# A 2048 x 2048 x 2048 matrix product with layer norm: the order of the first loads and products

## The chip, the cores and the metric

The kernel runs on one core of one Trainium2 chip. The metric is the device time of one execution in microseconds. A core has several engines, each with its own instruction queue: TensorE (PE in the profile; its weight loads are shown apart as PEld) does the matrix products, VectorE (DVE) and ScalarE (ACT) work elementwise, GpSimd (POOL) and SyncE (SP) here mostly issue transfers. An engine works through its queue in order and waits on semaphores that other engines or transfers raise. Transfers (DMA) are issued from a queue and then run beside the engines.

## The reference

```python
x = np.matmul(a, b)                       # a, b: 2048 x 2048, float32
mean = np.mean(x, axis=-1, keepdims=True)
var = np.var(x, axis=-1, keepdims=True)
normalized = (x - mean) / np.sqrt(var + eps)
return (gamma * normalized + beta).astype(np.float32)
```

The product has 16 x 16 x 4 = 1024 steps of 128 rows of A, 128 of K and 512 columns of B, each one TensorE instruction (called a product below). The inputs arrive as float32 and are multiplied as float16 with float32 sums.

## The kernel before

A is cut into 16 row tiles of 128 rows, B into 16 k tiles of 128 rows and 4 column blocks of 512 columns. Four k tiles make a chunk (KC = 4). Three things have to happen before a product can run: B's piece is loaded into a staging buffer (pool `stg`, 6 buffers of 1024 columns, or two halves of 512) and cast to float16 by VectorE; the row tile of A is loaded and cast likewise; and A is turned, since TensorE wants it with K on the partitions. In the first stage `turn` (L238) does that with TensorE: four transposes for each row tile and chunk into a PSUM bank, then one ScalarE copy back to SBUF. Products accumulate in PSUM, which has 8 banks; one bank holds one sum of 128 x 512 (`acc`), the result of one turn, or the target `warm` of the zero products. A bank goes to its next user when the engine that reads it is done.

All order is written out by hand (`manual_schedule`): each engine's queue is the order of the Python calls.

The first R = 5 row tiles (0 to 4) are worked together while B arrives, so that a piece of B serves five products. Their row pairs are [0, 1], [2, 3] and [4] (`pairs`, L208). The stages are:

- Opening (L269 to L286): block 0, k tiles 0 to 3, for the five rows, in the order in which the first pieces land: A row tile 0, B k tile 0, A row tiles 1 to 4, B k tiles 1, 2, 3 (`arrivals`, L163). `filler(n)` (L234) issues n products of zeros into the bank `warm`. After the stage the sums are put aside to SBUF by ScalarE (`put_aside`), which frees the banks.
- Blocks 1 and 2, k tiles 0 to 3 (L289 to L296), put aside likewise.
- Block 3, called MAIN, over all 16 k tiles (L299 to L315). Beside it the rows' next chunks are turned (`spots`, and the `turn` at L310). In its last chunk the rows finish one by one; `evacuate` (L90) copies the sum to SBUF on ScalarE and takes its statistics on VectorE, and `bring` (L250) issues the load and the cast of the next pieces of B (k tiles 4 to 15 of blocks 0, 1 and 2, 18 pieces in all).
- The rest of blocks 0, 1 and 2 (L318 to L328, L411 to L415): k tiles 4 to 15, added to what was put aside by VectorE (`add_rest`, L263).
- Row tiles 5 to 15 one after the other (L416 to L432), with all of B in SBUF; their A tiles are loaded with a cast from GpSimd's queue and turned by a transposing DMA from SP's queue. The normalisation of finished rows runs on VectorE from a backlog beside the products. After the last row only its own normalisation is left (`finish_row`).

The loads of the first stage are all issued on SP in the order of L216 to L230: the arrivals, blocks 1 and 2 of chunk 0, row pair 0 of chunk 1, and then, for each chunk c, the two pieces of block 3 (`load_b2`, two k tiles each, 512 KB) with the row pairs of chunk c + 1 between them (`load_pair`, 512 KB, or 256 KB for the single row tile 4). A load waits until its staging buffer has been cast, so both the issues on SP and the casts on VectorE follow this order.

Of the kernel before, what the change touches and what calls it, by code (L numbers as in the profile page):

```python
# [16 lines left out]
def kernel(  # L17
# [15 lines left out]
    n_kt = K // P  # L33
# [3 lines left out]
    KC = 4  # L37
    KW = KC * P
    n_kc = n_kt // KC
    R = 5  # L40
    ASIDE, MAIN = (0, 1, 2), 3
# [31 lines left out]
    def bank(name):  # L73
        return psum.tile([P, NB], FP32, tag="ps", name=name)
# [4 lines left out]
    def at(i):  # L79
        return pair[i // 2][:, i % 2]  # L80

    def mm(i, q, kt, first, last):
        if (i, q) not in acc:
            acc[i, q] = bank(f"acc{i}_{q}")
        nc.tensor.matmul(  # L85
            acc[i, q], at(i)[:, kt, :], b16[:, kt, ds(q * NB, NB)],
            start=first, stop=last,
        )

    def evacuate(i, q):  # L90
        if xs[i] is None:
            xs[i] = xpool.tile([P, N], FP32, tag="x", name=f"x{i}")
            bnst[i] = stat.tile([P, n_nb, 6], FP32, tag="bnst", name=f"bnst{i}")
        qs = ds(q * NB, NB)
        nc.scalar.copy(xs[i][:, qs], acc[i, q])  # L95
        nc.vector.bn_stats(bnst[i][:, q, :], xs[i][:, qs])  # L96
# [85 lines left out]
    def load_a1(i, c):  # L182
        st = half_stage()
        nc.sync.dma_start(st, a[ts(i, P), ts(c, KW)])  # L184
        a16_room(i, c)
        nc.vector.tensor_copy(a16_of[i, c], st)  # L186

    def load_a2(i, c):
        st = stg.tile([P, 2, NB], FP32, tag="st", name=f"sta{i}_{c}")
        nc.sync.dma_start(  # L190
            st, a[ds(i * P, 2 * P), ts(c, KW)].rearrange("(t p) k -> p t k", p=P))
        for m in (0, 1):
            a16_room(i + m, c)
        nc.vector.tensor_copy(held["a"][:, ds(i % KC, 2), :], st)  # L194
# [6 lines left out]
    def load_b2(k, q):  # L201
        st = stg.tile([P, 2, NB], FP32, tag="st", name=f"stb{q}_{k}")
        nc.sync.dma_start(
            st, b[ds(k * P, 2 * P), ds(q * NB, NB)].rearrange("(t p) n -> p t n", p=P))
        nc.vector.tensor_copy(b16[:, k:k + 2, ds(q * NB, NB)], st)  # L205
        return st

    pairs = [list(range(i, min(i + 2, R))) for i in range(0, R, 2)]  # L208

    def load_pair(j, c):  # L210
        if len(pairs[j]) == 2:
            load_a2(pairs[j][0], c)
        else:
            load_a1(pairs[j][0], c)
# [7 lines left out]
    for c in range(n_kc):  # L222
        load_b2(c * KC, MAIN)
        if c + 1 < n_kc:
            if c > 0:
                load_pair(0, c + 1)
            load_pair(1, c + 1)
        load_b2(c * KC + 2, MAIN)
        if c + 1 < n_kc:
            load_pair(2, c + 1)  # L230

    warm = bank("warm")

    def filler(n, to=None):  # L234
        for _ in range(n):
            nc.tensor.matmul(warm if to is None else to, zeros[:, 0:P], zeros, start=True, stop=True)  # L236

    def turn(rows, c):  # L238
        n = len(rows)
        t_ps = psum.tile([P, n, KC, P], FP16, tag="ps", name=f"tps{rows[0]}_{c}")  # L240
        for m, i in enumerate(rows):
            for j in range(KC):
                nc.tensor.transpose(t_ps[:, m, j, :], a16_of[i, c][:, ts(j, P)], ident)  # L243
        i0 = rows[0]
        nc.scalar.copy(  # L245
            pair[i0 // 2][:, ds(i0 % 2, n), ds(c * KC, KC), :], t_ps)
# [3 lines left out]
    def bring(n):  # L250
        for _ in range(n):
            k, q = later.pop(0)
            st = load_b2(k, q)
            if not later:
                nc.gpsimd.tensor_copy(gate, st[:, 0, 0:1])

    def put_aside(p, q):
        if xs[p] is None:
            xs[p] = xpool.tile([P, N], FP32, tag="x", name=f"x{p}")
            bnst[p] = stat.tile([P, n_nb, 6], FP32, tag="bnst", name=f"bnst{p}")  # L260
        nc.scalar.copy(xs[p][:, ds(q * NB, NB)], acc.pop((p, q)))  # L261
# [10 lines left out]
    mm(0, 0, 0, True, False)  # L272
    filler(1)
    turn([1], 0)
    filler(1)
    for i in range(2, R):
        filler(1)
        turn([i], 0)
        mm(i - 1, 0, 0, True, False)
    mm(R - 1, 0, 0, True, False)  # L280
    for kt in range(1, KC):
        filler(2 if kt == 1 else 0)
        for p in range(R):
            mm(p, 0, kt, False, kt == KC - 1)
            if kt == KC - 1:
                put_aside(p, 0)  # L286
# [12 lines left out]
    spots = {(0, 4): 0, (1, 1): 1, (1, 4): 2}  # L299
    for h in (0, 1):  # L300
        for p in range(R):
            for kt in (2 * h, 2 * h + 1):
                mm(p, MAIN, kt, kt == 0, False)
            if (h, p) in spots:
                turn(pairs[spots[h, p]], 1)
    for kt in range(KC, n_kt - KC):
        for p in range(R):
            mm(p, MAIN, kt, False, False)
        if kt % KC > 0:
            turn(pairs[kt % KC - 1], kt // KC + 1)  # L310
    for p, n in enumerate((0, 1, 0, 1, 1)):
        for kt in range(n_kt - KC, n_kt):
            mm(p, MAIN, kt, False, kt == n_kt - 1)
        bring(n)
        evacuate(p, MAIN)  # L315
# [152 lines left out]
```

## Time and profile before

| | us |
|---|---|
| median of 3 runs (lowest, highest) | 246.81 (246.68, 247.35) |
| profiled execution: its own time | 246.63 |
| profiled execution: span from first to last instruction | 244.6 |
| TensorE products, busy | 223.5 of 236.8 |
| VectorE busy | 175.2 |
| ScalarE busy | 52.6 |
| zero products (L236), 27: 19 in the opening, 8 behind the last row | 9.0 |
| transposes on TensorE (L243), 80 | 6.8 |
| casts of B in pieces of 1024 columns (L205), 30 of them, mean of one | 0.687 |

The page of a profile gives the span in parts: the busy time of each engine, the load of the DMA engines over time, the chain of work that ended last (followed back from the last instruction, at each step to what released it), and groups of instructions by line with what ended the idle time before them. The trace can also be asked for an engine's instructions in order of time (the timeline: start, duration, engine, line, operation, what it writes and reads, how many; in brackets the idle time before and what ended it), for all waits of one engine, and for the busy time of each engine in a stretch. Matmuls are pipelined: a product's bar is 0.38 us long, though one starts every 0.216 us.

Over the first 45 us the DMA engines move some 385 to 400 GB/s without a pause. The granted clock of TensorE is 1.00 in every stretch from 5.1 us on that was asked for.

### The profile page before, as it was taken

How to read it: one execution, taken by the hardware profiler on the slowest of the kernel's cores; microseconds unless marked ns; L12 is line 12 of the kernel's file. 1: busy time of each engine (PE TensorE's matmuls, PEld its weight loads, DVE VectorE, ACT ScalarE, POOL GpSimd, SP SyncE). 2: the span in 40 equal slices, each digit the busy share in tenths (PEclk: the TensorE clock that was granted, in tenths of full speed). 3: DMA queues.
4: the chain of work that ended last, by engine and by line, in shares of the span. 5: the costliest groups of instructions: out<-in, count | busy, mean ns of one | idle time of the engine just before them, and what ended most of it. 6: DMA issues, size and time to landing. Idle time of an engine off the chain costs nothing.

```text
span 244.6 us, 2975 instructions
## 1 busy us (share of the span) xinstructions
PE 236.8 (97%) x1137; PEld 108.0 (44%) x1137; DVE 175.2 (72%) x310; ACT 52.6 (21%) x96; POOL 7.2 (3%) x17
## 2 busy tenths in 40 slices
PE   7899999999999999999999999999999999999982
PEld 2344555444444444444444444444444444444430
DVE  1554554949997679999999995937557391947873
ACT  2457446400000011112111211112111211112100
POOL 0000000000300100000000000000000000000000
PEclk9999999999999999999999999999999999999996
DMA  4999999999999999899979897683907144120405
GB/s 125 398 386 385 388 387 385 316 357 375 331 271 179 158 131 201 196 316 205 263 189 283 147 298 222 149 200 71 256 4 190 68 123 137 74 97 0 175 1 172
DMA packets 41190, 52.64 MB, mean 215 GB/s; under 512 B 24404, under 2 KB 24404, under 8 KB 40920
## 3 DMA queue, kind: packets, MB, share of 16 engines
q1 hardware_dynamic: 39592, 46.68, 60.5%
q0 software_dynamic: 1584, 5.77, 15.4%
q8 instruction: 9, 0.15, 0.2%
q14 instruction: 5, 0.04, 0.0%
HBM read 35.67 MB, written 16.78 MB: 214 GB/s over the span
## 4 chain that ended last, share of the span: by engine, by line
PE 94%; DMA 2%; DVE 1%; ACT 0%; SPq 0%; issue 0%
PE acc L85 90%; DMA st<-in_a_dram 2%; PE tps L243 2%; PE w L380 1%; PE warm L236 1%; DVE x L390 0%; DVE bnst L364 0%; DVE x L367 0%; ACT at L245 0%; DVE a16s L186 0%; SPq L198 0%; PE nm_ps L375 0%; SPq L184 0%; DVE mv L102 0%; ACT lead L376 0%
## 5 line engine op out<-in xcount | busy, mean ns | idle before, releaser
L85 PE MATMUL acc<-b,at 128*128 128x512 f16 x1024 | 223.5, 379 | 0.7 <-DVE b L199 0.4
L85 PEld LDWEIGHTS <-at 128*128 128x128 f16 x1024 | 99.7, 98 | 119.7 <-ACT at L245 2.1
L96 DVE BATCH_NORM_STATS2 bnst<-x 128x6 f32<-128x512 f32 x48 | 33.0, 690 | 34.1 <-ACT x L95 33.9
L95 ACT COPY x<-acc 128x512 f32<-128x512 f32 x48 | 28.1, 586 | 107.8 <-PE acc L85 107.8
L117 DVE SCALAR_TENSOR_TENSOR x<-x,rstd,beta_b 128x512 f32<-128x512 f32 x61 | 43.1, 748 | 0.5
L111 DVE SCALAR_TENSOR_TENSOR x<-x,mv,gamma_b 128x512 f32<-128x512 f32 x60 | 42.1, 743 | 0.0
L205 DVE CAST b<-stb 128x1024 f16<-128x1024 f32 x30 | 20.4, 687 | 13.0 <-DMA stb<-in_b_dram 12.9
L106 ACT ACTIVATE sq<-ve 128x1 f32<-128x1 f32 x16 | 3.2, 203 | 55.5 <-DVE ve L104 55.5
L245 ACT COPY at<-tps 128x512 f16<-128x512 f16 (+1 forms) x14 | 10.8, 768 | 14.1 <-PE tps L243 14.0
L265 DVE TENSOR_TENSOR x<-acc,x 128x512 f32<-128x512 f32 x15 | 10.3, 686 | 3.0 <-PE acc L85 2.7
L266 DVE BATCH_NORM_STATS2 bnst<-x 128x6 f32<-128x512 f32 x15 | 10.4, 694 | 0.5
L236 PE MATMUL warm<-zeros 128*128 128x512 f16 x27 | 9.0, 463 | 1.2 <-DVE zeros L152 1.2
L340 POOL DMA_DIRECT2D a<-in_a_dram x11 | 6.4, 587 | 91.6 <-DMA at<-a 91.3
L261 ACT COPY x<-acc 128x512 f32<-128x512 f32 x15 | 7.6, 606 | 6.0 <-PE acc L85 6.0
L243 PEld LDWEIGHTS <-a16s 128*128 128x128 f16 x80 | 5.4, 98 | 4.7 <-DVE a16s L186 2.4
L243 PE MATMUL tps<-ident,a16s 128*128 128x128 f16 x80 | 6.8, 219 | 0.4 <-DVE a16s L186 0.3
L194 DVE CAST a16s<-sta 128x1024 f16<-128x1024 f32 x6 | 4.2, 694 | 4.0 <-DMA sta<-in_a_dram 4.0
L186 DVE CAST a16s<-st 128x512 f16<-128x512 f32 x8 | 3.4, 427 | 5.0 <-DMA st<-in_a_dram 4.8
L236 PEld LDWEIGHTS <-zeros 128*128 128x128 f16 x27 | 2.9, 113 | 4.6 <-issue 2.2
L102 DVE BATCH_NORM_AGGREGATE mv<-bnst 128x2 f32<-128x24 f32 x16 | 4.2, 264 | 0.5
L199 DVE CAST b<-st 128x512 f16<-128x512 f32 x4 | 1.7, 427 | 1.8 <-DMA st<-in_b_dram 1.8
L104 DVE TENSOR_TENSOR ve<-mv,eps_t 128x1 f32<-128x1 f32 x16 | 2.6, 160 | 0.5
(26 smaller groups left out, 16.9 us busy)
## 6 DMA issues: line engine op xcount, KB each, us to landing
stb<-in_b_dram SPq DMA_DIRECT2D x30, 512.0 KB, 6.5
out_dram<-x SPq DMA_DIRECT2D x30, 512.0 KB, 3.1
a<-in_a_dram POOLq DMA_DIRECT2D x11, 512.0 KB, 6.9
sta<-in_a_dram SPq DMA_DIRECT2D x6, 512.0 KB, 6.6
st<-in_a_dram SPq DMA_DIRECT2D x8, 256.0 KB, 6.3
st<-in_b_dram SPq DMA_DIRECT2D x4, 256.0 KB, 6.1
gamma_b<-in_gamma_dram SPq DMA_DIRECT2D x1, 1024.0 KB, 8.0
beta_b<-in_beta_dram SPq DMA_DIRECT2D x1, 1024.0 KB, 10.3
```

The source lines that it names most:

```text
L85: nc.tensor.matmul(acc[i, q], at(i)[:, kt, :], b16[:, kt, ds(q * NB, NB)], start=first, stop=last,)
L95: nc.scalar.copy(xs[i][:, qs], acc[i, q])
L96: nc.vector.bn_stats(bnst[i][:, q, :], xs[i][:, qs])
L111: nc.vector.scalar_tensor_tensor(xs[i][:, qs], xs[i][:, qs], mv[:, 0:1], gamma_b[:, qs], AluOp.subtract, AluOp.mult)
L117: nc.vector.scalar_tensor_tensor(xs[i][:, qs], xs[i][:, qs], rstd, beta_b[:, qs], AluOp.mult, AluOp.add)
L205: nc.vector.tensor_copy(b16[:, k:k + 2, ds(q * NB, NB)], st)
L236: nc.tensor.matmul(warm if to is None else to, zeros[:, 0:P], zeros, start=True, stop=True)
L243: nc.tensor.transpose(t_ps[:, m, j, :], a16_of[i, c][:, ts(j, P)], ident)
L245: nc.scalar.copy(pair[i0 // 2][:, ds(i0 % 2, n), ds(c * KC, KC), :], t_ps)
L261: nc.scalar.copy(xs[p][:, ds(q * NB, NB)], acc.pop((p, q)))
L265: nc.vector.tensor_tensor(xs[p][:, qs], acc[p, q], xs[p][:, qs], AluOp.add)
L266: nc.vector.bn_stats(bnst[p][:, q, :], xs[p][:, qs])
```

## The change

Four things are moved; what is computed, and how many loads, transposes and copies there are, stays.

- Loads: for chunks 1 and 2 the second piece of block 3 is issued ahead of row pair 1 (rows 2 and 3) of the next chunk instead of behind it.
- Opening: the order of the products, and the number of zero products. The k tile 1 products of rows 0 to 3 stand ahead of row 4's first product, and row 4's own k tile 1 product behind that. Between the turn of row 1 and the turn of row 2 there are two zero products as before; the ones behind that (one after row 1's and one after row 2's first product, two ahead of k tile 1) are gone.
- Turns beside block 3, chunks 1 and 2: row tile 4's turn moves from the end of the chunk's fourth k tile to behind that k tile's second product; the other two stay.
- Last chunk of block 3: its first two k tiles are done for all rows, k tile by k tile; then each row does its last two, is evacuated as before, and the three early calls of `bring` stand at rows 0, 1 and 3 instead of rows 1, 3 and 4.

```diff
     for c in range(n_kc):
         load_b2(c * KC, MAIN)
         if c + 1 < n_kc:
-            if c > 0:
-                load_pair(0, c + 1)
-            load_pair(1, c + 1)
+            load_pair(0 if c > 0 else 1, c + 1)
         load_b2(c * KC + 2, MAIN)
         if c + 1 < n_kc:
+            if c > 0:
+                load_pair(1, c + 1)
             load_pair(2, c + 1)
...
     mm(0, 0, 0, True, False)
     filler(1)
     turn([1], 0)
-    filler(1)
+    filler(2)
     for i in range(2, R):
-        filler(1)
         turn([i], 0)
         mm(i - 1, 0, 0, True, False)
+    for p in range(R - 1):
+        mm(p, 0, 1, False, False)
     mm(R - 1, 0, 0, True, False)
-    for kt in range(1, KC):
-        filler(2 if kt == 1 else 0)
+    mm(R - 1, 0, 1, False, False)
+    for kt in range(2, KC):
         for p in range(R):
             mm(p, 0, kt, False, kt == KC - 1)
             if kt == KC - 1:
...
+    spots = {(1, 4): 0, (2, 4): 1, (3, 1): 2}
     for kt in range(KC, n_kt - KC):
         for p in range(R):
             mm(p, MAIN, kt, False, False)
-        if kt % KC > 0:
-            turn(pairs[kt % KC - 1], kt // KC + 1)
-    for p, n in enumerate((0, 1, 0, 1, 1)):
-        for kt in range(n_kt - KC, n_kt):
+            if (kt % KC, p) in spots:
+                turn(pairs[spots[kt % KC, p]], kt // KC + 1)
+    for kt in range(n_kt - KC, n_kt - 2):
+        for p in range(R):
+            mm(p, MAIN, kt, False, False)
+    for p, n in enumerate((1, 1, 0, 1, 0)):
+        for kt in (n_kt - 2, n_kt - 1):
             mm(p, MAIN, kt, False, kt == n_kt - 1)
         bring(n)
         evacuate(p, MAIN)
```

## The prediction

> **What bounds the kernel now.** I read the chain that ended last first, because it says which engine sets the end, then the list of waits, then TensorE's timeline, then VectorE's.
>
> ```profile
> PE 94%; DMA 2%; DVE 1%; ACT 0%; SPq 0%; issue 0%
> ...
> PE warm L236 <- DVE zeros L152: 1.2, 1, 1.2
> PE acc L85 <- DVE b L199: 0.4, 1, 0.4
> PE acc L85 <- ACT at L245: 0.3, 1, 0.3
> PE tps L243 <- DVE a16s L186: 0.3, 1, 0.3
> ...
> 8.73 0.39 PE L85 MATMUL acc<-b,at 128*128 128x512 f16 x1
> 8.96 0.38 PE L236 MATMUL warm<-zeros 128*128 128x512 f16 x1
> 9.18 0.39 PE L243 MATMUL tps<-ident,a16s 128*128 128x128 f16 x4
> 9.41 0.39 PE L85 MATMUL acc<-b,at 128*128 128x512 f16 x1
> 9.63 0.38 PE L236 MATMUL warm<-zeros 128*128 128x512 f16 x1
> 9.85 0.39 PE L243 MATMUL tps<-ident,a16s 128*128 128x128 f16 x4
> 10.24 0.39 PE L85 MATMUL acc<-b,at 128*128 128x512 f16 x1
> 10.91 0.39 PE L85 MATMUL acc<-b,at 128*128 128x512 f16 x1 [0.28 <-ACT at L245]
> 11.14 0.59 PE L236 MATMUL warm<-zeros 128*128 128x512 f16 x2
> 11.57 14.19 PE L85 MATMUL acc<-b,at 128*128 128x512 f16 x65
> ```
>
> The four waits are all that TensorE has in the first 100 us, and the last of them ends at 10.91. From 11.57 on, by the chain, TensorE runs products and transposes without a hole to 235.03: one product starts every 0.216 us (65 of them between 11.57 and the next transposes at 25.60), four transposes take 0.22. So a rearrangement after 11.57 can win nothing by itself; it can only lose, or keep loads out of the way. What can be won lies before 11.57, where zero products still stand in the queue: four of them after 8.73.
>
> VectorE shows when each operand is ready:
>
> ```profile
> 8.53 0.43 DVE L186 CAST a16s<-st 128x512 f16<-128x512 f32 x1 [0.25 <-DMA st<-in_a_dram]
> 9.20 0.43 DVE L186 CAST a16s<-st 128x512 f16<-128x512 f32 x1 [0.25 <-DMA st<-in_a_dram]
> 9.89 0.43 DVE L199 CAST b<-st 128x512 f16<-128x512 f32 x1 [0.26 <-DMA st<-in_b_dram]
> ...
> 12.59 0.69 DVE L205 CAST b<-stb 128x1024 f16<-128x1024 f32 x1 [0.93 <-DMA stb<-in_b_dram]
> ...
> 35.35 0.69 DVE L205 CAST b<-stb 128x1024 f16<-128x1024 f32 x1 [0.66 <-DMA stb<-in_b_dram]
> 37.39 0.69 DVE L205 CAST b<-stb 128x1024 f16<-128x1024 f32 x1 [0.85 <-DMA stb<-in_b_dram]
> 38.74 0.69 DVE L205 CAST b<-stb 128x1024 f16<-128x1024 f32 x1 [0.66 <-DMA stb<-in_b_dram]
> ...
> 70.35 0.68 DVE L205 CAST b<-stb 128x1024 f16<-128x1024 f32 x1
> ```
>
> The first three are A rows 3 and 4 and B k tile 1, ready at 8.96, 9.63 and 10.32. Until then the loads set the pace: a 256 KB piece is cast every 0.68 us, a 512 KB piece every 1.36.
>
> **The opening, step by step.** Nothing differs up to row tile 1's first product at 8.73 (before: one and one zero product behind its transposes; after: two). From there:
> - Row 3's transposes no longer stand behind a zero product. They need the cast ending at 8.96; rows start 0.05 after their cast (7.61 to 7.66), so 9.01 instead of 9.18. They take 0.40 to the last result; ScalarE's copy, 0.03 behind, takes 0.58: 9.44 to 10.02 (after copy 2, ended at 9.35).
> - Row 2's product stays at 9.41: it waits for copy 2.
> - Row 4's transposes: cast 9.63, so 9.68 instead of 9.85; copy 4 runs 10.11 to 10.70.
> - Row 3's product: copy 3 plus 0.05, 10.07 instead of 10.24; TensorE is free at 10.29.
> - New: k tile 1 for rows 0 to 3. This is the added wait: B k tile 1's cast ends at 10.32, so 10.37, 10.58, 10.80, 11.02. Queued behind it is row 4's first product, now at 11.23 (copy 4 has been there since 10.70, so its old 0.28 us wait is covered), then row 4's k tile 1 at 11.45.
> - k tile 2 starts at 11.67. Before, it started at 11.57 + 5 x 0.216 = 12.65.
>
> The gain is 12.65 - 11.67 = **0.98 us**: four zero products (0.86) and 0.12 of waits. No row shows the new order. If the old waits behind the zero products reappear in full I get 0.86; if a step ahead of 10.37 were free, the four products' wait of 0.08 would go too, 1.06. I take 0.98, because the cast at 10.32 is a row that the change cannot move: the same loads in the same order stand ahead of it on SP.
>
> **What is late next.** Everything behind now asks 0.98 us earlier. Slacks, each the product's old start less its cast's end:
> - B column block 1, k 0-1: cast ends 13.28, used at 14.81 (11.57 + 15 products): 1.53, leaves 0.55; as its weight load stands one product ahead (0.22), 0.33 is safe.
> - MAIN k 10-11: cast ends 36.04, used 36.91: 0.87, which would *not* cover 0.98. The change loads it one A pair earlier: about 1.36 sooner, 34.69, leaving 1.24. The pair behind it comes 1.36 later, at 36.05 for transposes at 37.99 - 0.98 = 37.01. The same swap at k 6-7 leaves 1.9 and 1.6.
> - MAIN k 14-15: cast ends 39.43, used by row 0 at 39.74 + 0.43 = 40.17: 0.74, also too little. Taking k 12 and 13 for all rows first moves that use to 39.74 - 0.98 + 10 x 0.216 = 40.92, leaving 1.49. k 12 (38.08 for 38.76) keeps 0.68.
> - Row 4's transposes, three products earlier in each chunk: 37.89 in the last, for a cast ending at 36.54. Covered; their copy then ends sooner.
>
> So the edits of load order cost nothing as long as the loads keep this pace; without them some 0.1 to 0.25 us of the 0.98 would be stalled away again. On SP two B issues (0.37 us each) swap with two pair issues (0.37 to 0.46): the number, sizes and staging buffers asked for are the same. POOL gets nothing new; its one copy still waits for the last B piece.
>
> **The last chunk.** Rows now finish every 0.43 us instead of 0.86, faster than ScalarE's 0.58 (0.61 with the gap) per copy. Row 0's last product starts at 41.13, so copies run from 41.54 back to back to 44.6. The next block starts at 43.07 and needs five banks; the turned rows' three are free, the fourth (43.72) needs copy 0 (42.13) and the fifth copy 1 (42.73). Covered by over 1 us. If instead copies 2 and 3 were asked for, 43.95 against 43.72 would cost 0.2 to 0.3. On VectorE two bring calls now stand ahead of the first two statistics, so block 0's k 4-5, landed about 40.1, is cast at once rather than at 42.03; k 6-7 stands behind copy 0's statistics and ends about 43.4, used at 45.24.
>
> **The next thin place.** VectorE is nearly full from 53.4 to 71. The last B piece is cast at 70.35 to 71.03 and used at 72.12 (69.96 + 10 products): 1.09, leaves 0.11. That cast follows VectorE's own queue, so it does not come earlier with TensorE, but its queue starts with a load landing at 53.4 whose issue I expect no later. I cost it at zero; a delay d there costs about d - 0.1.
>
> [...] In the traced rows the nine first zero products take 4.02 us, 0.45 each, and those after 5.7 take 0.216; the granted clock is 1.00 from 5.1 on, through 5.10 to 8.51 where TensorE is busy for only 2.60 of 3.41 us. [...]
>
> **The sum.** The profiled execution took 246.63 us around a span of 244.6. Less 0.98: 245.65, span 243.6. It stands 0.18 below the median of the three runs, 246.81; against that, **245.8**. A difference under 0.3%, 0.74 us, can hardly be told from none.
>
> **Rivals.**
> 1. A load takes part of it back: block 1's first piece, k 12, or the last B piece, with 0.33, 0.68 and 0.11 to spare. For: DMA is full (385 to 390 GB/s) to 45 us. Against: order and sizes ahead of 13.3 are unchanged. A delay of 0.3 to 0.9 at the last piece returns 0.2 to 0.8: 246.0 to 246.6.
> 2. No change: the 0.98 comes back whole, where VectorE's full stretch holds TensorE to its old times. It needs that cast 1.1 us late: 246.8. Against: the casts ahead of it come earlier, not later.
> 3. Slower: TensorE's clock falls back in the thinner stretch from 8.96 to 10.37, where only 0.87 of 1.41 us is work. The slow stretch at the start lasted 1.20 to 5.1 and cost 0.45 - 0.22 = 0.23 per product; as long a stretch, 18 products at half rate for 3.9 us, costs 2.0, net +1.0: 247.8. It decides from 0.98 / 0.23, some four slow products. Against: holes are 0.18 us at most, and 5.10 to 8.51 was no fuller.
>
> **How the numbers follow.** Full gain (0.86 to 1.06): 0.68. Rival 1: 0.17, a sixth of it under 0.24 us of loss and so still faster. Rival 2: 0.08. Rival 3 and other losses: 0.07. Faster by over 0.3%: 0.68 + 0.03 = 0.71; within: 0.22; slower: 0.07. The range takes the bound of 1.06 and the runs' spread below the median (0.13), 246.81 - 1.06 - 0.13 = 245.6, a little lower for the unseen, 245.5, up to rival 1's 246.6. The likeliest case alone: 245.6 to 246.0.
>
> **What would show it.** TensorE's k tile 2 from about 11.67 and no wait in the list longer than 0.4 us after that; B k tile 1 named as the releaser at 10.37; the last product's end near 234.05. A wait on a B cast near 13.6, 38.8 or 71 means rival 1; products of 0.43 us after 8.5, rival 3; k tile 2 at 12.6 would show my reading of the opening wrong.

## The result and the profile after

The changed kernel took 246.07 us (median of 22 runs), the kernel before 246.95 us in the same comparison: a ratio of 0.9964, 95% interval 0.9956 to 0.9971, that is 0.88 us less. The profiled execution has a span of 244.0 us, 0.6 below that of before.

The list of TensorE's waits in the first 100 us after has two lines where before had four:

```profile
PE warm L236 <- DVE zeros L152: 1.2, 1, 1.2
PE acc L85 <- DVE b L199: 0.9, 1, 0.9
```

The 0.9 is row 0's first product, waiting for B k tile 0. Nothing new has appeared further back. TensorE's timeline after, from the same place on (start, duration, what it writes and reads, how many):

```profile
7.26 0.38 PE L85 MATMUL acc<-b,at 128*128 128x512 f16 x1 [0.89 <-DVE b L199]
...
9.03 0.39 PE L85 MATMUL acc<-b,at 128*128 128x512 f16 x1
9.30 0.40 PE L243 MATMUL tps<-ident,a16s 128*128 128x128 f16 x4
9.71 0.39 PE L85 MATMUL acc<-b,at 128*128 128x512 f16 x1
9.98 0.40 PE L243 MATMUL tps<-ident,a16s 128*128 128x128 f16 x4
10.38 14.69 PE L85 MATMUL acc<-b,at 128*128 128x512 f16 x67
24.91 0.61 PE L243 MATMUL tps<-ident,a16s 128*128 128x128 f16 x8
```

The zero products are gone from between the transposes and the products, and the run of 67 products starts at 10.38 with row 3's first one; its one hole is 0.07 us ahead of the second product, which waits for B k tile 1's cast (10.61). VectorE's timeline after shows the casts that released them, and the one at the far end:

```profile
6.78 0.43 DVE L199 CAST b<-st 128x512 f16<-128x512 f32 x1 [1.51 <-DMA st<-in_b_dram]
...
8.82 0.43 DVE L186 CAST a16s<-st 128x512 f16<-128x512 f32 x1 [0.23 <-DMA st<-in_a_dram]
9.50 0.43 DVE L186 CAST a16s<-st 128x512 f16<-128x512 f32 x1 [0.25 <-DMA st<-in_a_dram]
10.18 0.43 DVE L199 CAST b<-st 128x512 f16<-128x512 f32 x1 [0.26 <-DMA st<-in_b_dram]
...
69.66 0.68 DVE L205 CAST b<-stb 128x1024 f16<-128x1024 f32 x1
```

All casts from B k tile 0 on are 0.3 us later than in the execution before (10.18 against 9.89), although nothing ahead of them was changed. This is the load's own scatter: the cast of B k tile 0 ended between 6.85 and 7.28 in the eleven profiles shown in the table below, and the kernel before (6.90) is near the early end. So two profiles must not be compared by the clock on the wall but from a cast. B k tile 1's cast ends at 10.61; k tile 2's first product, the eighth of that run, starts at 11.96, 1.35 us later. Before it was 10.32 and 12.65, 2.33 later. The difference is 0.98 us, as forecast; 0.3 of it is hidden in this one pair of profiles by the late load.

For the experiments two distances are used, both read from the trace: **k tile 2** is the time from the end of B k tile 1's cast to the first product of k tile 2; **whole** is the time from the end of B k tile 3's cast to the start of the last product of the kernel. They leave the scatter of the first loads out.

| kernel | k tile 2 | whole | gain in whole | median us (before beside it) | ratio, 95% interval |
|---|---|---|---|---|---|
| before | 2.33 | 222.98 | | 246.95 | |
| changed | 1.35 | 221.98 | 1.00 | 246.07 (246.95) | 0.9964, 0.9956 to 0.9971 |
| e1 opening only | 1.35 | 222.28 | 0.70 | 246.21 (247.02) | 0.9961, 0.9945 to 0.9978 |
| e2 all but the opening | 2.36 | 222.99 | -0.01 | 246.80 (247.02) | 0.9996, 0.9981 to 1.0012 |
| e3 fewer zeros only | 1.76 | 222.40 | 0.58 | 246.35 (247.02) | 0.9975, 0.9960 to 0.9990 |
| e4 order only | 1.90 | 222.54 | 0.44 | 246.51 (247.02) | 0.9975, 0.9961 to 0.9990 |
| e5 no more zeros | 1.88 | 222.51 | 0.47 | 247.12 (246.90) | 0.9997, 0.9978 to 1.0016 |
| e7 old last chunk | 1.34 | 222.32 | 0.66 | 246.20 (246.90) | 0.9970, 0.9959 to 0.9981 |
| e8 old loads | 1.34 | 223.03 | -0.05 | 246.17 (246.90) | 0.9976, 0.9962 to 0.9991 |
| e9 changed again | 1.34 | 221.98 | 1.00 | 245.84 (246.88) | 0.9955, 0.9942 to 0.9967 |
| e10 B earlier | (other order) | 221.82 | 1.16 | 245.81 (246.88) | 0.9958, 0.9943 to 0.9973 |

The times alone cannot tell 0.2 us apart (0.08%; half an interval is 0.08 to 0.2%); the two distances can, but each is one execution.

### The profile page after: what moved, and what is told of

Same layout as the page of the kernel before. It is cut to its first block, busy times and chain, and to the rows that moved or that the text cites. A ratio compares the mean times of both kernels' runs of the same rounds, so it can differ in the third digit from the quotient of the medians.

```text
span 244.0 us, 2967 instructions
## 1 busy us (share of the span) xinstructions
PE 236.1 (97%) x1133; PEld 107.7 (44%) x1133; DVE 175.3 (72%) x310; ACT 52.0 (21%) x96; POOL 7.0 (3%) x17
## 4 chain that ended last, share of the span: by engine, by line
PE 94%; DMA 2%; DVE 1%; SPq 0%; issue 0%; ACT 0%
PE acc L85 91%; DMA st<-in_a_dram 2%; PE tps L243 2%; PE w L385 1%; DVE x L395 0%; DVE bnst L369 0%; DVE x L372 0%; DVE a16s L186 0%; PE warm L236 0%; SPq L198 0%; SPq L184 0%; PE nm_ps L380 0%; DVE mv L102 0%; ACT lead L381 0%; DVE nm L377 0%
## 5 line engine op out<-in xcount | busy, mean ns | idle before, releaser
L245 ACT COPY at<-tps 128x512 f16<-128x512 f16 (+1 forms) x14 | 10.6, 770 | 14.1 <-PE tps L243 13.8
L266 DVE BATCH_NORM_STATS2 bnst<-x 128x6 f32<-128x512 f32 x15 | 10.4, 694 | 0.5
L236 PE MATMUL warm<-zeros 128*128 128x512 f16 x23 | 7.7, 478 | 1.2 <-DVE zeros L152 1.2
```

What stands on the lines that cost most here:

```text
L245: nc.scalar.copy(pair[i0 // 2][:, ds(i0 % 2, n), ds(c * KC, KC), :], t_ps)
L266: nc.vector.bn_stats(bnst[p][:, q, :], xs[p][:, qs])
```

## The experiments

**e1: the opening alone.** The kernel before with the opening of the change, and its old loads, turns and last chunk.

```diff
-    filler(1)
+    filler(2)
     for i in range(2, R):
-        filler(1)
         turn([i], 0)
         mm(i - 1, 0, 0, True, False)
+    for p in range(R - 1):
+        mm(p, 0, 1, False, False)
     mm(R - 1, 0, 0, True, False)
-    for kt in range(1, KC):
-        filler(2 if kt == 1 else 0)
+    mm(R - 1, 0, 1, False, False)
+    for kt in range(2, KC):
```

> The changed opening alone, with the old load order, the old turns and the old last chunk. Theory: k tile 2 starts 1.35 us after B k tile 1's cast ends (before 2.33, after 1.35), a gain of 0.98 us, but TensorE then waits for two casts of block 3: about 0.16 at k 10-11 (slack 0.87 less 0.05 for the start less 0.98) and about 0.13 more at k 14-15 (slack 0.74 less 0.05, with 0.82 left). Net gain about 0.69. Rival (the moved loads and the new last chunk do nothing): no such waits, gain 0.98.

Measured: k tile 2 at 1.35, whole 0.70 better. TensorE's timeline of e1 at block 3's k 10, where the old load order has the A pair ahead of B:

```profile
35.54 0.61 PE L243 MATMUL tps<-ident,a16s 128*128 128x128 f16 x8
36.19 1.24 PE L85 MATMUL acc<-b,at 128*128 128x512 f16 x5
```

Eight transposes take 0.45 from start to next start everywhere else (36.47 to 36.91 for the same ones before); here 0.65. TensorE stood 0.20 us for the cast, which the timeline of VectorE in e1 puts here:

```profile
35.44 0.69 DVE L205 CAST b<-stb 128x1024 f16<-128x1024 f32 x1 [0.65 <-DMA stb<-in_b_dram]
```

It ends at 36.13, 0.06 ahead of the product. A second hole of 0.09 stands at k 14-15 (two products 0.31 apart). Together 0.29, as expected (0.16 and 0.13). So the opening makes the gain, and the moved loads and the new last chunk keep 0.3 us of it.

**e2: everything but the opening.** The changed kernel with the old opening (the diff of e1 the other way round).

> Everything but the opening: new load order, new turns, new last chunk, with the old opening. Theory: TensorE has no hole behind 11.57 to close, so the gain is 0.0, within 0.15 us. Rival (part of the measured 0.88 us comes from here): 0.2 us or more faster, the opening worth that much less.

Measured: whole 222.99 against 222.98, ratio 0.9996 with 1 inside the interval. The rest wins nothing by itself. The rival (0.2 us or more from here) is out by this one profile; by the times alone 0.2 us, 0.08%, would still fit the interval.

**e3: fewer zeros only,** and **e4: order only.** The changed kernel with one half of the opening undone.

```diff
 # e3: k tile 1 behind row 4's first product again
-    for p in range(R - 1):
-        mm(p, 0, 1, False, False)
     mm(R - 1, 0, 0, True, False)
-    mm(R - 1, 0, 1, False, False)
-    for kt in range(2, KC):
+    for kt in range(1, KC):
...
 # e4: the four zero products again in their old places
-    filler(2)
+    filler(1)
     for i in range(2, R):
+        filler(1)
         turn([i], 0)
         mm(i - 1, 0, 0, True, False)
+    filler(2)
     for p in range(R - 1):
```

> The changed kernel with the four zero products gone, but k tile 1 behind row 4's first product as before. Theory: row 4's product waits for its copy to about 10.75, k tile 2 starts 1.72 us after B k tile 1's cast: gain 0.61, so the order is worth 0.37. Rival (the zero products alone are what cost): 0.86 to 0.98, k tile 2 at 1.35 to 1.47.

> The changed kernel with the four zero products put back, in their old places (ahead of the turns of rows 3 and 4, two ahead of k tile 1). Theory: k tile 2 starts 1.86 us after B k tile 1's cast: gain 0.47, so the zero products are worth 0.51 of the 0.98. Rival (the order alone is what counts, the zeros lie in waits): 0.98, k tile 2 at 1.35.

Measured: e3 0.57 by k tile 2 (2.33 - 1.76), e4 0.43 (2.33 - 1.90), each 0.04 less than expected. Neither rival holds. The two halves add up to 1.00 against 0.98 for both. e3 keeps the old wait of row 4's product on its copy; its list of waits has

```profile
PE acc L85 <- ACT at L245: 0.3, 1, 0.3
```

which neither e4 nor the changed kernel has: the products of k tile 1 lie over that copy.

**e5: no zero products behind the first nine.**

```diff
-    filler(3)
     mm(0, 0, 0, True, False)
-    filler(1)
     turn([1], 0)
-    filler(2)
     for i in range(2, R):
```

> The changed kernel without any zero product behind the first nine (six more gone, between row 0's turn and row 2's). They all lie in waits for loads. Theory (the clock holds through a thin stretch): k tile 2 again 1.35 us after B k tile 1's cast, all products 0.216 apart, time as the changed kernel, within 0.15. Rival (the clock falls when TensorE is busy for only about 0.7 of the 3.4 us from 5.1 to 8.5): products 0.43 apart somewhere behind 8.5, 1 to 2 us slower than the changed kernel.

Measured: ratio 0.9997, so by the medians the whole gain is lost: 247.12 against 246.07 and 245.84 for the changed kernel. TensorE's timeline of e5:

```profile
5.44 0.61 PE L243 MATMUL tps<-ident,a16s 128*128 128x128 f16 x4 [0.23 <-DVE a16s L186]
6.95 0.59 PE L85 MATMUL acc<-b,at 128*128 128x512 f16 x1 [0.90 <-DVE b L199]
7.65 1.28 PE L243 MATMUL tps<-ident,a16s 128*128 128x128 f16 x8
8.94 0.61 PE L85 MATMUL acc<-b,at 128*128 128x512 f16 x1
9.34 0.63 PE L243 MATMUL tps<-ident,a16s 128*128 128x128 f16 x4
9.76 0.63 PE L85 MATMUL acc<-b,at 128*128 128x512 f16 x1
10.19 0.58 PE L243 MATMUL tps<-ident,a16s 128*128 128x128 f16 x4
10.65 3.63 PE L85 MATMUL acc<-b,at 128*128 128x512 f16 x16
```

Four transposes take 0.6 where they take 0.40 after, one product 0.6 for 0.38, up to 10.6; the products from 10.65 are at full rate (16 in 3.63 us, 0.216 apart). The trace's record of the granted clock has full speed from 10.59 us here, from 5.10 before and 5.29 after. So my theory that the zeros only fill waits is wrong for these six. In this execution the rival had the right cause with the wrong picture: the clock did not fall in a thin stretch, it came up later (10.59 for 5.29), and that cost 0.53 (k tile 2 at 1.88 for 1.35).

The median lost more, 1.05 against the changed kernel's first one, and this execution does not stand for it: it took 246.20 us at a mean granted clock of 0.990. Eight of the other eleven took 246.5 to 247.4 at a mean of 0.983 to 0.986, which no run of the kernel before or of the changed one has (0.987 or more). The clock column reads 1.00 for e5 from 0 to 5 and from 5 to 8.5 us too, where its instructions run slowly, so a late start of full speed alone does not lower this mean. A further 3.41 us at half clock would lower it by 0.007 (an estimate: half of 3.41 / 244, where 3.41 us is the step by which the recorded lengths of full speed differ, see the last section). That fits the rival's fall behind an early start of full speed, but none of these eight has a trace. The late start is shown once; the fall in the others is likely, and not shown.

**e6 and e10: B k tiles 1 and 2 ahead of A row tiles 3 and 4.** Two runs of the same kernel; the first one's profiled execution is told of below, under the hardware.

```diff
-    arrivals = [("a", 0), ("b", 0)] + [("a", i) for i in range(1, R)]
-    arrivals += [("b", k) for k in range(1, KC)]
+    arrivals = [("a", 0), ("b", 0), ("a", 1), ("a", 2), ("b", 1), ("a", 3),
+                ("b", 2), ("a", 4), ("b", 3)]
...
     filler(2)
-    for i in range(2, R):
-        turn([i], 0)
-        mm(i - 1, 0, 0, True, False)
-    for p in range(R - 1):
-        mm(p, 0, 1, False, False)
-    mm(R - 1, 0, 0, True, False)
-    mm(R - 1, 0, 1, False, False)
+    turn([2], 0)
+    for p, kt in ((1, 0), (0, 1), (1, 1), (2, 0), (2, 1)):
+        mm(p, 0, kt, kt == 0, False)
+    turn([3], 0)
+    for p in (0, 1, 2):
+        mm(p, 0, 2, False, False)
+    turn([4], 0)
+    for kt in (0, 1, 2):
+        mm(3, 0, kt, kt == 0, False)
...
```

Row 4's four products and k tile 3 follow, row by row.

> The changed kernel with B k tiles 1 and 2 loaded ahead of A row tiles 3 and 4 and the products ordered to match. Theory (the order in which loads land, not TensorE, sets the opening): seven products instead of four are done or under way when TensorE first runs without holes; block 1 starts 1.97 us after the cast of B k tile 3 instead of 2.17; 0.2 us faster than the changed kernel. Rival (rows 3 and 4, turned later, become the wait): block 1 at 2.17 or later, no gain.

> B k tiles 1 and 2 loaded ahead of A row tiles 3 and 4, once more, since the profile of the first run shows an execution at a TensorE clock of 0.56 from end to end. Theory (the order in which loads land sets the opening): block 1 starts 1.97 us after the cast of B k tile 3 (changed kernel 2.16), 0.2 us faster than the changed kernel, unless a later load takes it back. Rival (rows 3 and 4, turned later, become the wait): 2.16 or more, no gain.

Measured: e6 246.28 us, ratio 0.9969 (0.9958 to 0.9981). In e10 block 1 starts at 13.96, B k tile 3's cast ends at 11.98: 1.98, expected 1.97, and 0.17 earlier than the 2.15 of e9. Whole is 0.16 better than e9. TensorE's timeline of e10:

```profile
9.07 1.29 PE L85 MATMUL acc<-b,at 128*128 128x512 f16 x5
10.20 0.39 PE L243 MATMUL tps<-ident,a16s 128*128 128x128 f16 x4
10.70 0.81 PE L85 MATMUL acc<-b,at 128*128 128x512 f16 x3
11.36 0.40 PE L243 MATMUL tps<-ident,a16s 128*128 128x128 f16 x4
11.59 13.33 PE L85 MATMUL acc<-b,at 128*128 128x512 f16 x61
```

Six products are under way before 10.2, where the changed kernel has three; the one hole over 0.1 us from there on is 0.28 at 10.4, for B k tile 2. So in this execution the order in which pieces land sets the opening, as expected. In time this cannot be told from the changed kernel (245.81 against 245.84 beside it): 0.17 us is 0.07%.

**e7: the old last chunk.** Changed kernel, block 3's last four k tiles row by row.

```diff
-    for kt in range(n_kt - KC, n_kt - 2):
-        for p in range(R):
-            mm(p, MAIN, kt, False, False)
-    for p, n in enumerate((1, 1, 0, 1, 0)):
-        for kt in (n_kt - 2, n_kt - 1):
+    for p, n in enumerate((0, 1, 0, 1, 1)):
+        for kt in range(n_kt - KC, n_kt):
```

> The changed kernel with the old last chunk of block 3 (row by row over four k tiles). Theory: row 0's product at k 14 waits about 0.29 us for its cast (slack 0.74 less 0.05 less 0.98), so 0.29 slower than the changed kernel. Rival: no wait there, same time.

The two ends of the hole in e7's timeline of TensorE:

```profile
38.35 1.24 PE L85 MATMUL acc<-b,at 128*128 128x512 f16 x5
39.78 20.45 PE L85 MATMUL acc<-b,at 128*128 128x512 f16 x94 [0.18 <-DVE b L205]
```

Five products last from 38.35 to 39.43; the sixth starts at 39.78. The hole is 0.34 (expected 0.29) and whole is 0.34 worse than the changed kernel's.

**e8: the old order of loads.** Changed kernel with the first diff hunk undone.

> The changed kernel with the old order of loads in chunks 1 and 2. Theory: a wait of about 0.16 us at block 3's k 10-11 (slack 0.87 less 0.05 less 0.98), none at k 6-7; 0.16 slower than the changed kernel. Rival: no wait, same time.

TensorE's timeline of e8 at k 10-11:

```profile
35.86 0.61 PE L243 MATMUL tps<-ident,a16s 128*128 128x128 f16 x8
36.43 1.24 PE L85 MATMUL acc<-b,at 128*128 128x512 f16 x5
```

From start to start it is 0.57 in place of 0.45, a hole of 0.12 (expected 0.16). This one execution also shows what I had called the next thin place. VectorE's and TensorE's timelines of e8:

```profile
51.11 0.69 DVE L205 CAST b<-stb 128x1024 f16<-128x1024 f32 x1 [0.62 <-DMA stb<-in_b_dram]
54.58 0.69 DVE L205 CAST b<-stb 128x1024 f16<-128x1024 f32 x1 [2.77 <-DMA stb<-in_b_dram]
...
71.28 0.68 DVE L205 CAST b<-stb 128x1024 f16<-128x1024 f32 x1
```

```profile
68.83 2.97 PE L85 MATMUL acc<-b,at 128*128 128x512 f16 x13
72.01 10.95 PE L85 MATMUL acc<-b,at 128*128 128x512 f16 x50 [0.22 <-DVE b L205]
83.34 1.04 PE L85 MATMUL acc<-b,at 128*128 128x512 f16 x4 [0.38 <-DMA at<-a]
```

One load landed at 54.6 (52.65 after), VectorE's full stretch began 1.9 late, its last cast ended at 71.96, and TensorE stood 0.38 for it and then 0.54 for row tile 5's transposes: this execution took 247.09 us, the median of e8's twelve is 246.17. Why that load was late is not settled; the old load order, over by 40 us, is not shown to be the cause.

**e9: the changed kernel again,** beside e10.

> The changed kernel unaltered, beside the next run. Theory: k tile 2 again 1.35 us after B k tile 1's cast, block 1 2.16 after the cast of B k tile 3, 0.7 to 1.0 us faster than before.

Measured: 0.9955 and 1.04 us (246.88 - 245.84), a little over the 0.7 to 1.0 expected; the distances are those of the first profile.

## Why the prediction was right, point by point

Forecast 245.8 us, range 245.5 to 246.6; measured 246.07. Against the medians of the same comparison the gain is 0.88 (246.95 - 246.07) for the 0.98 forecast, and the interval 0.9956 to 0.9971 (0.72 to 1.09 us) holds it.

- *The opening, step by step.* Each start came where the steps put it, shifted by the 0.3 of the late load: row 3's transposes 9.30 (9.01 forecast), row 2's product 9.71 (9.41), row 4's transposes 9.98 (9.68), row 3's product 10.38 (10.07), k tile 2 at 11.96 (11.67). The bound by the cast of B k tile 1 was right.
- *Four zeros 0.86 and 0.12 of waits.* The sum was right, the split a matter of the way one counts: alone the zeros are worth 0.57, the order 0.43.
- *What is late next.* Slacks at k 10-11 and k 14-15 were sized within 0.1: e1, e7 and e8 show the holes that the moved loads and the new last chunk avoid. The 0.1 to 0.25 that I gave for both together is 0.3 in e1, since I left the 0.05 from cast to product out. (The loads move 383 to 402 GB/s from 6 to 45 us; from 0 to 3 and from 3 to 6 us it is 70 and 170, so "over the first 45 us" was too wide. No slack rests on it.)
- *The last chunk* costs nothing, as costed; ScalarE's five copies run back to back (from 41.84, 2.54 us for five). Their start is as forecast, with the 0.3; my 3.1 us for five was too long, since copies that follow each other start every 0.48, not every 0.61.
- *The next thin place* was mis-sized: 0.11 of slack forecast, 1.1 in the profile after (the last cast ends at 70.33, and its product starts at 72.12 - 0.69 = 71.43). The step that failed is "so it does not come earlier with TensorE". VectorE's full stretch starts behind the cast of one load, which I took to land no later than before. Counted from the end of B k tile 3's cast, that cast starts 41.7 us later before, 40.7 after, 41.0 in e1 (the opening alone) and 42.1 in e2 (all but the opening). So in these four it came earlier with the opening, and not with the moved `bring` calls, which e2 has too. How the earlier products bring that load forward no run took apart, and it scatters: the other kernels with the whole opening have 40.4 to 41.3, but e8 42.5.
- *Rival 1* is seen in one execution of e8, which has the old loads, and neither in the changed kernel's profiles nor in its median. *Rival 2* is out. *Rival 3* did not happen, but "against: 5.10 to 8.51 was no fuller" was the wrong argument: that the clock, at 1.00 from 5.10 on, stayed there through a stretch with 2.60 of 3.41 us of work says nothing about a clock that has not come up yet. In e5, without the six zero products left in the opening, it came up at 10.59, and by the medians the gain is gone. No run shows by what rule the clock falls or comes up; that thin work lets it fall was my estimate. The price was put together wrongly too: in 3.9 us at half rate there is room for nine products (0.427 apart), not 18; the 2.0 us is right.
- *Granted clock.* The rows that I read as "1.00 from 5.1 on" say 1.00 for the first 3 us too, where zero products start 0.427 apart. For the first microseconds that column can't be read; the spacing of the instructions can.

## What to carry to other kernels

Find the first moment from which the bounding engine runs without a hole: here a reordering behind it only protected (e2, all but the opening: -0.01 us by itself), and the gain was bounded by what stood before it. When everything behind is then asked for earlier, list the slack of each load against the gain; two here were too small, and moving them was worth 0.3 of 1.0 us. Zero products that lie in waits may still be paying for the clock: without six of them e5 had full speed from 10.59 instead of 5.29 us. Take out those that stand ahead of work that is ready, and look at the spacing of the instructions before taking out the others.

## What the runs showed of the hardware

- The clock record of the traces has full speed from 5.10 (before), 5.29 (changed), 6.64 (e1), 6.90 (e3) and 10.59 us (e5), for 235.52, 235.52, 232.11, 232.11 and 228.69 us. The lengths differ by 3.41 us and by twice that. The same nine zero products stand ahead of it in all five kernels (from 1.2 us on, 0.427 us apart in the profiles before and after), and in e5 six others are gone. What decides the moment was not shown. Once there, the clock stayed at full speed to 240.62 us (before) and 240.81 (changed), also from 5.10 to 8.51, where TensorE is busy for 2.60 of 3.41 us before, and from 5.29 to 8.70, where it is busy for 2.38 of 3.41 in the changed kernel. How thin a stretch it holds through is open: with full speed from 5.1, about 26% of the 3.41 us behind that would be work in e5 (an estimate: three turns of 0.22 and one product of 0.216 in 3.41 us), and eight of its runs have a mean clock of 0.983 to 0.986, as a fall there would give by the estimate under e5.
- e1 lost nothing to its later start of full speed, 6.64 us (k tile 2 at 1.35, as after). e3, with 6.90, shows no loss that stands out either: its 1.76 misses the expected 1.72 by 0.04, as e4's 1.90 does 1.86, with full speed from 5.35.
- One execution of the kernel with B earlier took 423.49 us, with a granted clock of 0.56 from 4.5 us to the end and products about 0.40 us apart. The 16 other executions of the same kernel took 245.5 to 246.7. So the kernel alone does not account for it; the cause is open.
